# Starting the next stage's products inside the last attention half-head of a fp32 encoder layer

## The chip, the cores and the metric

One core of one Trainium2 chip runs the whole kernel in one launch. The metric is the device time of a run in microseconds (us); three runs of the kernel before were timed.

## The reference, cut to what matters

One encoder layer is applied to two request groups (512 tokens each, model width 1024) with shared weights, all in fp32:

```
h  = rmsnorm(x);  u = h @ w_in                        # one combined projection
hm = mlstm(q, k, v, gates)                            # branch A, both directions
y_m = (sigmoid(o) * rmsnorm(hm)) @ w_mo               # its projection, 1024 x 1024
p  = softmax(q k^T) per head;  o = p @ v              # branch B, 8 heads
y_a = o @ w_ao                                        # its projection, 1024 x 1024
x  = x + (sigmoid(g_m) * y_m + sigmoid(g_a) * y_a) @ w_out
x  = x + (silu(h2 @ w_gate) * (h2 @ w_up)) @ w_down   # FFN
x  = x + sigmoid(x @ w_ple_gate) * (p_l @ w_ple);  y = rmsnorm(x)
```

The stretch that matters is the end of branch B's attention and the start of `@ w_mo`, which is followed by `@ w_ao`.

## The kernel before, in words

Tiles are 128 partitions by 512 fp32 values. To keep fp32 accuracy every operand is split in two fp32r parts (`hi`, a cast on ScalarE; `lo`, source minus `hi` on VectorE, helper `lo_of`, line 155), and a product is three matmuls per 128 rows: hi·hi, hi·lo, lo·hi. `E`, `S`, `V`, `GP` are TensorE, ScalarE, VectorE and GpSimd.

**Attention.** There are 16 half-heads (`NU`; 8 heads times 2 groups). Each iteration `u` of the loop makes the scores of half-head u (`score`: five matmuls into a bank `sc` and a maximum on VectorE, for each of four query blocks), their exponentials (`expo`, ScalarE), transposes them (`turn`: four transposes into a bank `pt`, a cast `aph` on ScalarE; `turn_lo`: `apl` on VectorE), projects keys and queries of half-head u+1 (`proj_hi`, banks `pj`), and multiplies the weights of half-head u-1 with its values (`weigh`: eight `aph` and four `apl` matmuls into the bank `av`). Division by the softmax sum is done late for half-heads below `EVEN` = 14: `sums_row(u-1)` takes the reciprocals `rc`, transposes them on TensorE, and sends them through DRAM on GpSimd's DMA queue to come back broadcast as the tile `rb`; `weighed(u-1)` multiplies `av` by `rb` into `oz` at the end of the same iteration. Half-heads 14 and 15 divide `p` itself (`inverse`, `even`). The iteration of u = 15 has an order of its own (`if last:`) and a further one, u = 16, finishes it. Inside the loop `pinned` is set: compute instructions keep program order on each engine. Outside it a planner, which simulates a timeline, orders the instructions. `fill(...)` places small side jobs in the loop: splits of `hops`, the operands of the next stage.

**Next stage.** `w_mo` and then `w_ao` are applied as 2 x 2 block products with seven instead of eight block multiplications (class `Seven`). A quad is one such block pair: products P1, P2, P7, P6, P5, Q4, P3, each 12 matmuls, into banks b0, b1, b2; `w_mo` and `w_ao` have four quads each. Operand sums come from `Ops.part` (lines 934 to 956), weight sums from `Seven.source` (lines 999 to 1016), on VectorE for mo quads 0 and 3 and ao quad 0, on GpSimd for the others. `outputs` and `put_z` take results out of the banks. `chain` issues the products in an order with operands needed four products ahead. Weights of quad 0's P1, P2 and P7 are split during the loop (`ahead`); everything else of the chain is issued behind the loop (`issue_after(anchors)`). Before the chain the loop's banks are closed and six banks b0, b1, b2 and a spare are opened.

`hops`' raw tiles are loaded again for P5, Q4, P3 (`X2`), and for these its sums are made on GpSimd:

```
    hops.r, hops.t, hops.sums = {}, {}, lambda n: GP
    hops.raw = lambda g, k: load(hzd[g][k], X2, "x")
```

Of the kernel before, what the change touches and what calls it, by code (L numbers as in the profile page):

```python
# [17 lines left out]
NB = T // P  # L18
# [44 lines left out]
def encoder_kernel(ctx: ExitStack, tc: tile.TileContext, a):  # L63
# [56 lines left out]
            t = self.tags[n]  # L120
            return self.pool.tile([P, T], F32, name=nm(n), tag=t, bufs=self.bufs[t])

    pb = [None]

    def banks(name, bufs, **tags):
        if pb[0]:
            pb[0].ctx.close()
        pb[0] = Banks(name, bufs, tags) if name else None

    def bank(n="mm"):  # L130
        return pb[0](n)

    banks("P1", dict(mm=3, sc=2, tp=2, bc=1), mm="mm", sc="sT nm", tp="ssc tpc vtp ht", bc="rbc")
# [564 lines left out]
    M2.close()  # L698
    M1.close()
    MC.close()  # L700
    banks("P2", dict(pj=2, sc=3, tp=2, av=1), pj="mm pj", sc="sc", tp="pt", av="av")
    Q = Slots("Q", vt=1, rb=1, qkv=12, qst=4, p=4, ph=1, pl=1)
    QL = Slots("QL", lat=16)
    lat = {}
# [154 lines left out]
    def even(u, i):  # L859
        x = att[u]  # L860
        S.activation(out=x["p"][i], in_=x["p"][i], func=AF.Copy, scale=x["rc"][:, i : i + 1])
# [26 lines left out]
    def weigh(u):  # L888
        x, (vh, vl) = att[u], vn[u]
        ob = x["ob"] = bank("av")  # L890
        for j in range(NB):
            c = slice(j * P, (j + 1) * P)
            E.matmul(ob, vh[:, c], x["ph"][:, j], start=j == 0, stop=False)
            E.matmul(ob, vl[:, c], x["ph"][:, j], start=False, stop=False)
        for j in range(NB):
            E.matmul(ob, vh[:, j * P : (j + 1) * P], x["pl"][:, j], start=False, stop=j == NB - 1)

# [17 lines left out]
    late = {}  # L915
# [5 lines left out]
    class Ops:  # L921
# [2 lines left out]

        def __init__(self, raw, tmp, sums):
            self.raw, self.tmp, self.sums = raw, tmp, sums
            self.r, self.t, self.x = {}, {}, {}

        def get(self, n, k):
            if (n, k) not in self.r:  # L930
# [1 line left out]
            return self.r[n, k]  # L932

        def part(self, name, k):
            if name in ("P1", "P2", "P3"):
                return self.get({"P1": "a", "P2": "c", "P3": "d"}[name], k)
            add = self.sums(name).tensor_tensor
            if name == "P7":
                t = self.t[k] = self.tmp() or self.get("b", k)
                add(out=t, in0=self.get("b", k), in1=self.get("d", k), op=ALU.subtract)  # L940
            elif name == "P6":
                t = self.t[k]
                add(out=t, in0=t, in1=self.get("a", k), op=ALU.subtract)  # L943
            elif name == "P5":
                t = self.get("a", k)
                add(out=t, in0=t, in1=self.get("b", k), op=ALU.subtract)
            elif k in self.t:
                t = self.t[k]
                add(out=t, in0=t, in1=self.get("c", k), op=ALU.add)
            else:  # L950
                t = self.get("c", k)
                add(out=t, in0=t, in1=self.get("a", k), op=ALU.subtract)
                add(out=t, in0=t, in1=self.get("d", k), op=ALU.subtract)
            return t
# [27 lines left out]
    class Seven:  # L982
# [43 lines left out]
            self.w[name] = (hi, lo)  # L1026
            return (lambda: S.copy(hi, src)), (lambda: lo_of(lo, src, hi))

        def product(self, name):
            if name == "P6" and "P7" not in self.w:  # L1030
                self.w["P7"] = self.weights("P7")
            if name not in self.w:
                self.w[name] = self.weights(name)
            whi, wlo = self.w[name]
            b, first = {"P1": ("b1", 1), "P6": ("b1", 0), "P5": ("b1", 0), "P3": ("b1", 0), "P2": ("b0", 1),
                        "P7": ("b2", 1), "Q4": ("b2", 0)}[name]
            if first:
                self.bk[b] = bank(b)
            bk = self.bk[b]
            sk = dict(skip_group_check=True)  # L1040
            for k in range(self.kh):
                c = slice(k * P, (k + 1) * P)
                hi, lo = self.ops.x[name][k]
                E.matmul(bk, whi[:, c], hi, start=bool(first) and k == 0, stop=False, **sk)  # L1044
                E.matmul(bk, whi[:, c], lo, start=False, stop=False, **sk)  # L1045
                E.matmul(bk, wlo[:, c], hi, start=False, stop=k == self.kh - 1, **sk)  # L1046
            self.out(name, self.bk)

    def chain(quads, head=False, look=4, made=()):

        order = [(0, n) for n in ("P1", "P2", "P7")]
        if head:
            order = [(0, "P1"), (0, "P2"), (1, "P1"), (1, "P2"), (0, "P7"), (0, "P6"), (0, "P5"), (0, "Q4"), (1, "P7"), (0, "P3")]
        full = ("P6", "+P1", "P5", "+P2", "Q4", "+P7", "P3")
        ends = {
            len(quads) - 3: ("P6", "+P1", "P5", "+P2", "Q4", "P3"),
            len(quads) - 2: ("P6", "P7", "P5", "+P1", "Q4", "P3"),
            len(quads) - 1: ("P6", "P7", "P5", "P2", "Q4", "P3"),
        }
        for i in range(1 if head else 0, len(quads)):  # L1060
            for n in ends.get(i, full):
                if n[0] != "+":
                    order.append((i, n))
                elif i + 1 < len(quads):
                    order.append((i + 1, n[1:]))
        made = dict(made)

        def make(i):
            if i not in made:
                made[i] = quads[i][1]()  # L1070

        for at, (q, n) in enumerate(order):
            for i, m in order[at : at + look + 1]:
                quads[i][0].need(m)
            for i, _ in order[at : at + 2]:
                make(i)
            made[q].product(n)

    def outputs(put):
        keep = {}  # L1080

        def out(name, bk):
            if name in ("P1", "P6", "P5"):
                t = late["OP"]("ev", "u")
                S.copy(t, bk["b1"])  # L1085
                keep[name] = t
            if name in ("P2", "P5", "Q4"):
                t = keep[{"P2": "P1", "P5": "P5", "Q4": "P6"}[name]]
                b = bk["b0" if name == "P2" else "b2"]
                V.tensor_tensor(out=t, in0=b, in1=t, op=ALU.add if name == "P2" else ALU.subtract)  # L1090
                put({"P2": (0, 0), "P5": (1, 1), "Q4": (1, 0)}[name], t)
            if name == "P3":
                put((0, 1), bk["b1"])

        return out
# [77 lines left out]
    quads = [pair("mo", c, hops, put_z(c)) for c in range(4)]  # L1173
    ahead, anchors = {}, []

    def ahead_hi(n):
        hi, ahead[n] = pairs[0].ahead(n)
        hi()

    def ahead_lo(n):  # L1180
        ahead[n]()

    pinned[0] = True
    for u in range(NU + 1):
# [69 lines left out]
            todo_["f"] = [(ahead_lo, "P1")]  # L1254
        if u == 14:
            todo_ = {"mid": [(ahead_hi, "P2")], "d": [(ahead_lo, "P2")], "late": [(ahead_hi, "P7")], "f": [(ahead_lo, "P7")]}

        def odd(v, i):
            if EVEN <= v < NU - 1:
# [3 lines left out]
        if last:  # L1263
            score(u, 0)
            expo(u, 0)
            score(u, 1)
            turn(u - 1, 3)
            turn_lo(u - 1, 3)
            expo(u, 1)
            score(u, 2)  # L1270
            inverse(u, 0)
            even(u, 0)
            expo(u, 2)
            score(u, 3)
            inverse(u, 1)
            even(u, 1)
            expo(u, 3)
            for i in (2, 3):
                inverse(u, i)
                even(u, i)  # L1280
            v_split(u)
            weigh(u - 1)
            weighed(u - 1)
            for i in range(NB - 1):
                turn(u, i)
                turn_lo(u, i)
            continue
        if now:
            score(u, 0)
        fill("a")  # L1290
        if now:
            expo(u, 0)
# [8 lines left out]
        if then:  # L1301
            if u - 1 < EVEN:
                V.reciprocal(out=att[u - 1]["rc"], in_=att[u - 1]["den"])
            turn_lo(u - 1, 3)
        odd(u, 0)
        fill("c")
        if nxt:
            proj_hi(kn, u + 1, "ckv", 512)
            proj_lo(kn, u + 1)
        if then and u - 1 < EVEN:  # L1310
            sums_row(u - 1)
        odd(u, 1)
        fill("mid")
        fill("d")
        if then:
            weigh(u - 1)
        if now:
# [1 line left out]
            v_load(u + 1)  # L1319
            turn(u, 0)  # L1320
            turn_lo(u, 0)
            score(u, 2)
            turn(u, 1)
            expo(u, 2)
            turn_lo(u, 1)
# [7 lines left out]
            expo(u, 3)  # L1333
            turn_lo(u, 2)
            odd(u, 3)
            if then:
                weighed(u - 1)
            fill("f")
            fill("end")
        else:  # L1340
# [6 lines left out]
        if u == NU - 2:  # L1347
            QL.close()
            X2 = Slots("X2", "right", x=16)
    pinned[0] = False  # L1350
    hops.r, hops.t, hops.sums = {}, {}, lambda n: GP
    hops.raw = lambda g, k: load(hzd[g][k], X2, "x")
    Q.close()
    late["OP"] = Slots("OP", h=24, sg=4, ev=8)


    yr = [[None] * KD for _ in range(G)]
    banks("PF", dict(b1=3, b0=2, b2=2, sp=1), b0="b0", b1="b1", b2="b2", sp="sp")

    def put_y(c):  # L1360
        def put(at, t):
# [11 lines left out]
    with ExitStack() as behind:  # L1373
        for i in anchors:
            behind.enter_context(tc.issue_after(i))
        quads += [pair("ao", c, oops, put_y(c)) for c in range(4)]
        chain(quads, made=pairs)


    y = [[None] * KD for _ in range(G)]  # L1380
# [6 lines left out]
            V.scalar_tensor_tensor(out=lo, in0=t, scalar=0.5, in1=hi.bitcast(F32), op0=ALU.mult, op1=ALU.subtract)  # L1387
            y[g][k] = (hi, lo)
    OP = late["OP"]
    banks("P3", dict(mm=5, tp=1, bc=2), mm="mm", tp="ssc", bc="rbc")  # L1390

    class Sl:

# [423 lines left out]
```

## Time and profile before

| | |
|---|---|
| time, median of 3 runs | 1884.51 us (1883.68 to 1887.18) |
| profiled execution, its time | 1885.22 us |
| its span, first to last instruction | 1883.4 us |
| mean granted TensorE clock | 0.990 |
| PE (TensorE matmul) busy | 1831.4 us, 97% |
| VectorE (DVE) busy | 1238.8 us, 66% |
| ScalarE (ACT) busy | 860.7 us, 46% |
| GpSimd (POOL) busy | 393.3 us, 21% |

A timeline row has start (us from the span's start), duration, engine, line, operation, out<-in, count, and in brackets the idle time before it with what ended it. Rows merge neighbouring instructions of one kind. The page ends matmuls by a model, so the distance between the starts of two matmuls is the better measure of a matmul. In the loop most lines are L79, the helper that pins instructions, so tile names tell what is what. A row of a window has the busy time of each engine with its count of instructions, then the granted clock, the DMA share and GB/s.

### The profile page before, as it was taken

To read this page: it belongs to the slowest core of one execution; us is meant where nothing else is said; L and a number is where in the kernel's file an instruction comes from. 1 tells how busy PE (TensorE), PEld (TensorE's weight loads), DVE (VectorE), ACT (ScalarE), POOL (GpSimd) and SP (SyncE) were. 2 spreads that over 40 slices of the span, in tenths; PEclk is the share of its full clock that TensorE was granted. 3 is DMA by queue.
4 is the path that set the end of the run, shared out by engine and by line. 5 is a ranking of instruction groups with operands and counts; after the bars stand their busy time and mean duration, and the time that the engine had idled before them with its cause. 6 is when DMAs were issued, how large, how long until landed. Compare 5 with 4: busy or idle time off the path is not lost.

```text
span 1883.4 us, 24476 instructions
## 1 busy us (share of the span) xinstructions
PE 1831.4 (97%) x8815; PEld 1525.6 (81%) x8815; DVE 1238.8 (66%) x2084; ACT 860.7 (46%) x1690; POOL 393.3 (21%) x316
## 2 busy tenths in 40 slices
PE   9999999999999999987999999999999999999996
PEld 7889898988888777766878888888888888888786
DVE  6757576766532377768898588444444469878756
ACT  6255555653322566663444356333333344434433
POOL 0101000100000022215131002666556623111000
PEclk9999999999999999998999999999999999999998
DMA  4211212122333444354665342233222347533342
GB/s 165 66 59 49 69 44 79 44 69 79 121 113 111 156 124 118 96 201 157 193 209 155 120 145 84 101 115 110 96 97 95 130 142 237 166 129 101 105 136 95
DMA packets 104217, 220.43 MB, mean 117 GB/s; under 512 B 12584, under 2 KB 23264, under 8 KB 104096
## 3 DMA queue, kind: packets, MB, share of 16 engines
q1 hardware_dynamic: 88592, 166.15, 26.6%
q10 hardware_dynamic: 12096, 43.00, 7.1%
q0 software_dynamic: 3408, 9.73, 1.6%
q8 instruction: 69, 1.13, 0.3%
q14 instruction: 52, 0.43, 0.1%
HBM read 160.37 MB, written 54.26 MB: 114 GB/s over the span
## 4 chain that ended last, share of the span: by engine, by line
PE 47%; DVE 7%; issue 1%; ACT 1%; DMA 0%; ACTq 0%; DVEq 0%; POOLq 0%
PE b L1044 12%; PE b L1046 12%; PE b L1045 12%; PE mm L79 2%; DVE wp L155 2%; DVE xl L155 1%; PE mm L186 1%; PE mm L184 1%; PE mm L185 1%; PE mm L1606 1%; PE mm L1607 1%; PE mm L1608 1%; ACT p L79 0%; DVE x L1543 0%; DVE t L943 0%
## 5 line engine op out<-in xcount | busy, mean ns | idle before, releaser
L1046 PE MATMUL b<-xh,wp 128*128 128x512 f32 x1148 | 443.7, 391 | 12.2 <-DVE wp L155 12.2
L1045 PE MATMUL b<-xl,wp 128*128 128x512 f32 x1148 | 446.0, 390 | 2.1 <-DVE xl L155 2.1
L1044 PE MATMUL b<-xh,wp 128*128 128x512 f32 x1148 | 439.9, 391 | 6.5 <-ACT u L1085 2.3
L978 ACT CAST wp<-wst 128x512 fp32r<-128x512 f32 (+1 forms) x268 | 163.2, 612 | 301.0 <-PE b L1046 250.1
L155 DVE TENSOR_TENSOR wp<-wst,wp 128x512 fp32r<-128x512 f32 (+1 forms) x268 | 248.1, 928 | 68.9 <-ACT wp L978 68.7
L1046 PEld LDWEIGHTS b<-xh,wp 128*128 128x128 f32 x1148 | 216.3, 188 | 58.8 <-DVE wp L155 13.8
L1044 PEld LDWEIGHTS b<-xh,wp 128*128 128x128 f32 x1148 | 216.3, 188 | 57.1 <-ACT u L1085 5.5
L1045 PEld LDWEIGHTS b<-xl,wp 128*128 128x128 f32 x1148 | 216.1, 188 | 47.5 <-DVE xl L155 2.9
L184 PE MATMUL mm<-hh,whi 128*128 128x512 f32 x560 | 219.5, 392 | 0.9 <-DVE ql L155 0.9
L185 PE MATMUL mm<-hl,whi 128*128 128x512 f32 x560 | 219.2, 391 | 0.0
L186 PE MATMUL mm<-hh,wlo 128*128 128x512 f32 x560 | 218.9, 391 | 0.0
L1090 DVE TENSOR_TENSOR u<-b,u 128x512 f32<-128x512 f32 x90 | 61.8, 688 | 130.9 <-PE b L1046 82.1
L184 PEld LDWEIGHTS mm<-hh,whi 128*128 128x128 f32 x560 | 105.5, 188 | 23.0 <-DVE ql L155 1.3
L186 PEld LDWEIGHTS mm<-hh,wlo 128*128 128x128 f32 x560 | 105.6, 188 | 22.2 <-DVE wlo L155 0.3
L185 PEld LDWEIGHTS mm<-hl,whi 128*128 128x128 f32 x560 | 105.5, 188 | 21.3
L1005 POOL TENSOR_TENSOR s<-wst,wst 128x512 f32<-128x512 f32 (+1 forms) x29 | 45.3, 1562 | 308.7 <-DMA wst<-wd 137.0
L169 ACT CAST whi<-wst 128x1024 fp32r<-128x1024 f32 x59 | 62.0, 1050 | 98.6 <-PE mm L185 58.7
L1085 ACT COPY u<-b 128x512 f32<-128x512 f32 x90 | 50.7, 589 | 106.8 <-PE b L1046 64.0
L1505 POOL TENSOR_TENSOR sg<-sg,u 128x512 f32<-128x512 f32 x30 | 54.5, 1818 | 202.1 <-DVE u L1090 202.1
L155 DVE TENSOR_TENSOR wlo<-wst,whi 128x1024 fp32r<-128x1024 f32 (+2 forms) x62 | 75.0, 1212 | 14.5 <-ACT whi L169 13.6
L155 DVE TENSOR_TENSOR xl<-ld,xh 128x512 fp32r<-128x512 f32 x105 | 77.9, 769 | 1.0 <-ACT xh L1536 0.5
L383 DVE TENSOR_TENSOR tg<-rs,mm 128x512 f32<-128x512 f32 x32 | 22.0, 686 | 82.8 <-PE mm L186 77.6
(383 smaller groups left out, 3582.7 us busy)
## 6 DMA issues: line engine op xcount, KB each, us to landing
wst<-w SPq DMA_DIRECT2D x73, 512.0 KB, 3.2
wst<-w ACTq DMA_DIRECT2D x60, 512.0 KB, 3.8
ld<-actd SPq DMA_DIRECT2D x77, 256.0 KB, 3.4
actd<-t SPq DMA_DIRECT2D x40, 256.0 KB, 2.9
x<-x SPq DMA_DIRECT2D x32, 256.0 KB, 4.0
ld<-hzd SPq DMA_DIRECT2D x32, 256.0 KB, 3.0
wst<-wd ACTq DMA_DIRECT2D x16, 512.0 KB
actd<-sg SPq DMA_DIRECT2D x30, 256.0 KB, 2.3
```

The source lines that it names most:

```text
L155: e.tensor_tensor(out=out, in0=src, in1=hi.bitcast(F32), op=ALU.subtract)
L169: S.copy(hi[:, :n], st[:, :n])
L184: E.matmul(bk, whi[:, c], hi, start=k == 0, stop=False)
L185: E.matmul(bk, whi[:, c], lo, start=False, stop=False)
L186: last_mm[0] = E.matmul(bk, wlo[:, c], hi, start=False, stop=k == nk - 1)
L978: S.copy(hi, src)
L1044: E.matmul(bk, whi[:, c], hi, start=bool(first) and k == 0, stop=False, **sk)
L1045: E.matmul(bk, whi[:, c], lo, start=False, stop=False, **sk)
L1046: E.matmul(bk, wlo[:, c], hi, start=False, stop=k == self.kh - 1, **sk)
L1085: S.copy(t, bk["b1"])
L1090: V.tensor_tensor(out=t, in0=b, in1=t, op=ALU.add if name == "P2" else ALU.subtract)
L1505: e.tensor_tensor(out=sg[at], in0=sg[at], in1=t, op=ALU.mult)
```

## The change

The loop's two banks `pj` become two named banks `l0`, `l1` in a pool of their own (`low`), which stays open through the `w_mo` and `w_ao` stage. In iteration 15 and 16 the first four products of quad 0 (P1, P2, P7, P6) are issued between the attention's own TensorE work: P1 after the last score, P2 after the first transposed block, P7 after the second, P6 after the fourth. P1 and P6 go into `l0`, P7 into `l1`, P2 into a bank of the tag `sc`. With them come P1's and P2's results, P6's weights, the weights of quad 1's P1 and P2, and P5's four operand sums, all pinned. The chain then starts with quad 1's P1, P2, P7 and goes on with quad 0's P5, Q4, P3.

All sums of `hops` are now on VectorE (the line that switched them to GpSimd is gone). The 16 raw tiles are loaded at the end of iteration 14. In every iteration `sums_row` moves into `weigh`, between its eight `aph` and its four `apl` matmuls, and `weighed` moves from the end of the iteration to behind the first score of the next. For half-head 14 the third score moves ahead of `weigh`, and the normalisation of block 1 ahead of the key projection.

```diff
+    LOW = dict(mm=("l0", "l1"), pj=("l0", "l1"), b1=("l0", None, None), b2=("l1", None, None))
...
-    banks("P2", dict(pj=2, sc=3, tp=2, av=1), pj="mm pj", sc="sc", tp="pt", av="av")
+    banks("P2", dict(sc=3, tp=2, av=1), under=("l0", "l1"), sc="sc b0", tp="pt", av="av")
...
     def weigh(u):
...
+        if u < EVEN:
+            sums_row(u)
         for j in range(NB):
             E.matmul(ob, vh[:, j * P : (j + 1) * P], x["pl"][:, j], start=False, stop=j == NB - 1)
...
     def chain(quads, head=False, look=4, made=(), done=()):
...
-            for n in ends.get(i, full):
+            for n in ends.get(i, ("+P1", "+P2", "+P7", "P5", "Q4", "P3") if (i, "P6") in done else full):
...
+        order = [o for o in order if o not in done]
...
         if last:
...
             score(u, 1)
+            weighed(u - 2)
             turn(u - 1, 3)
...
             even(u, 1)
+            pre("P1", False)
             expo(u, 3)
...
             weigh(u - 1)
+            pairs[0].out("P1", pairs[0].bk)
+            ahead_hi("P6")
+            ahead_lo("P6")
+            turn(u, 0)
+            turn_lo(u, 0)
+            pre("P2")
+            turn(u, 1)
+            turn_lo(u, 1)
+            for k in range(4):
+                hops.pre["P5", k] = hops.part("P5", k)
             weighed(u - 1)
-            for i in range(NB - 1):
-                turn(u, i)
-                turn_lo(u, i)
+            pre("P7")
+            ahead_hi("P1", 1)
+            ahead_lo("P1", 1)
+            turn(u, 2)
+            turn_lo(u, 2)
+            ahead_hi("P2", 1)
+            ahead_lo("P2", 1)
             continue
         if now:
             score(u, 0)
+            if u > 1:
+                weighed(u - 2)
...
         odd(u, 0)
+        odd(u, 1)
         fill("c")
...
-        if then and u - 1 < EVEN:
-            sums_row(u - 1)
-        odd(u, 1)
         fill("mid")
         fill("d")
+        if now and u >= EVEN:
+            score(u, 2)
+        if u == NU:
+            pre("P6", False)
         if then:
             weigh(u - 1)
...
-            if then:
-                weighed(u - 1)
             fill("f")
...
             X2 = Slots("X2", "right", x=16)
+            hops.r, hops.t = {}, {}
+            hops.raw = lambda g, k: load(hzd[g][k], X2, "x")
+            for x in "abcd":
+                for k in range(4):
+                    hops.get(x, k)
     pinned[0] = False
-    hops.r, hops.t, hops.sums = {}, {}, lambda n: GP
...
-    banks("PF", dict(b1=3, b0=2, b2=2, sp=1), b0="b0", b1="b1", b2="b2", sp="sp")
+    banks("PF", dict(b1=2, b0=2, b2=2), b0="b0", b1="b1", b2="b2")
...
-        chain(quads, made=pairs)
+        pairs[0].out("P6", pairs[0].bk)
+        chain(quads, made=pairs, done=[(0, n) for n in ("P1", "P2", "P7", "P6")])
```

More of the change, by code (lines that the diff above doesn't have):

```diff
@@ L121, in __call__, with banks @@
             return self.pool.tile([P, T], F32, name=nm(n), tag=t, bufs=self.bufs[t])
-    pb = [None]
-    def banks(name, bufs, **tags):
+    pb, low, turns = [None], [None], {}
+    def banks(name, bufs, under=None, **tags):
         if pb[0]:
             pb[0].ctx.close()
+        if under is not None:
+            if low[0]:
+                low[0].ctx.close()
+            low[0] = Banks(name + "L", {n: 1 for n in under}, {n: n for n in under}) if under else None
+            turns.clear()
         pb[0] = Banks(name, bufs, tags) if name else None
+    LOW = dict(mm=("l0", "l1"), pj=("l0", "l1"), b1=("l0", None, None), b2=("l1", None, None))
     def bank(n="mm"):
+        if low[0] and n in LOW:
+            key = "pj" if n == "mm" else n
+            i = turns[key] = turns.get(key, -1) + 1
+            at = LOW[n][i % len(LOW[n])]
+            if at:
+                return low[0](at)
         return pb[0](n)
@@ L926, in __init__ @@
             self.raw, self.tmp, self.sums = raw, tmp, sums
-            self.r, self.t, self.x = {}, {}, {}
+            self.r, self.t, self.x, self.pre = {}, {}, {}, {}
         def get(self, n, k):
@@ L934, in part @@
         def part(self, name, k):
+            if (name, k) in self.pre:
+                return self.pre.pop((name, k))
             if name in ("P1", "P2", "P3"):
@@ L1027, in ahead, with product @@
             return (lambda: S.copy(hi, src)), (lambda: lo_of(lo, src, hi))
-        def product(self, name):
+        def product(self, name, out=True):
             if name == "P6" and "P7" not in self.w:
@@ L1046, in product, with chain @@
                 E.matmul(bk, wlo[:, c], hi, start=False, stop=k == self.kh - 1, **sk)
-            self.out(name, self.bk)
-    def chain(quads, head=False, look=4, made=()):
+            if out:
+                self.out(name, self.bk)
+    def chain(quads, head=False, look=4, made=(), done=()):
         order = [(0, n) for n in ("P1", "P2", "P7")]
@@ L1083, in out @@
             if name in ("P1", "P6", "P5"):
-                t = late["OP"]("ev", "u")
+                t = late["OP"]("ev", "u") if "OP" in late else Q("qkv", "u")
                 S.copy(t, bk["b1"])
@@ L1174, in encoder_kernel, with ahead_hi, ahead_lo @@
     ahead, anchors = {}, []
-    def ahead_hi(n):
-        hi, ahead[n] = pairs[0].ahead(n)
-        hi()
-    def ahead_lo(n):
-        ahead[n]()
+    def ahead_hi(n, i=0):
+        hi, ahead[i, n] = pairs[i].ahead(n)
+        hi()
+    def ahead_lo(n, i=0):
+        ahead[i, n]()
     pinned[0] = True
@@ L1256, in encoder_kernel @@
             todo_ = {"mid": [(ahead_hi, "P2")], "d": [(ahead_lo, "P2")], "late": [(ahead_hi, "P7")], "f": [(ahead_lo, "P7")]}
+        pre = lambda name, out=True: pairs[0].product(name, out)
         def odd(v, i):
@@ L1321, in encoder_kernel @@
             turn_lo(u, 0)
-            score(u, 2)
+            if u < EVEN:
+                score(u, 2)
             turn(u, 1)
@@ L1349, in encoder_kernel @@
             X2 = Slots("X2", "right", x=16)
+            hops.r, hops.t = {}, {}
[3 more added lines that the diff above has]
+                    hops.get(x, k)
     pinned[0] = False
-    hops.r, hops.t, hops.sums = {}, {}, lambda n: GP
-    hops.raw = lambda g, k: load(hzd[g][k], X2, "x")
     Q.close()
@@ L1389, in encoder_kernel @@
     OP = late["OP"]
-    banks("P3", dict(mm=5, tp=1, bc=2), mm="mm", tp="ssc", bc="rbc")
+    banks("P3", dict(mm=5, tp=1, bc=2), under=(), mm="mm", tp="ssc", bc="rbc")
     class Sl:
```

## The prediction

> **What bounds the kernel now.** I began with the page: which engine is full, and where it is not.
>
> ```profile
> PE 1831.4 (97%) x8815; PEld 1525.6 (81%) x8815; DVE 1238.8 (66%) x2084; ACT 860.7 (46%) x1690; POOL 393.3 (21%) x316
> ...
> PE   9999999999999999987999999999999999999996
> ...
> PEclk9999999999999999998999999999999999999998
> ```
>
> TensorE is the bound nearly everywhere, so only time in which it stands or runs at a lower clock can be won. Slices 18 and 19 (about 800 to 894 us) are the weakest in the middle, and the granted clock sinks there too. Next the waits of PE alone:
>
> ```profile
> PE b L1046 <- DVE wp L155: 12.2, 3, 10.9
> PE pt L79 <- DVE rc L79: 4.3, 11, 1.0
> PE pt L79 <- DVE apl L79: 3.0, 1, 3.0
> ...
> PE pt L79 <- ACT p L79: 1.4, 2, 0.7
> PE av L79 <- ACT aph L79: 0.9, 2, 0.7
> ```
>
> Columns: total, times, longest. The first row holds one wait of 10.9 us for a weight's lo part; the second is small and frequent, in the attention loop; the third is one wait of 3.0. The windows from the last half-head on place them (busy us of PE, PEld, DVE, ACT, POOL, then the clock):
>
> ```profile
> 836.00:848.00 12.00, 8.99 (x45) 6.98 (x43) 6.23 (x15) 8.62 (x19) 1.11 (x2) 0.89 0.91 327
> 848.00:855.00 7.00, 6.33 (x21) 4.99 (x21) 3.02 (x5) 2.11 (x4) 0.53 (x1) 0.70 0.08 9
> ...
> 862.00:874.00 12.00, 1.13 (x4) 0.88 (x4) 12.00 (x3) 0.27 (x1) 10.70 (x10) 0.66 0.17 45
> 874.00:880.00 6.00, 6.00 (x23) 4.84 (x22) 5.97 (x9) 0.00 (x0) 1.22 (x1) 0.82 0.07 24
> ...
> 945.00:955.00 10.00, 10.00 (x46) 8.11 (x44) 10.00 (x13) 5.06 (x10) 4.09 (x3) 1.00 0.33 92
> 955.00:970.00 15.00, 11.37 (x39) 7.91 (x39) 15.00 (x25) 7.78 (x16) 5.54 (x3) 0.89 0.90 296
> ```
>
> There are two holes, each followed by a stretch at half clock: one in the last half-head, one from 862 to 873. A third, smaller one at 955 to 970, where w_ao follows w_mo, has VectorE busy throughout. The timeline of PE shows the first two from inside:
>
> ```profile
> 839.42 0.39 PE L79 MATMUL av<-aph,vh 128*128 128x512 f32 x1
> ...
> 842.17 1.03 PE L79 MATMUL pt<-ident,p 128*128 128x128 f32 x8
> 846.20 1.97 PE L79 MATMUL pt<-ident,p 128*128 128x128 f32 x8 [2.99 <-DVE apl L79]
> 848.84 0.79 PE L79 MATMUL av<-aph,vh 128*128 128x512 f32 x1 [0.68 <-ACT aph L79]
> ...
> 853.28 0.40 PE L1044 MATMUL b<-xh,wp 128*128 128x512 f32 x1
> ...
> 861.45 0.39 PE L1044 MATMUL b<-xh,wp 128*128 128x512 f32 x1
> 861.67 0.39 PE L1045 MATMUL b<-xl,wp 128*128 128x512 f32 x1
> 872.93 0.80 PE L1046 MATMUL b<-xh,wp 128*128 128x512 f32 x1 [10.87 <-DVE wp L155]
> ...
> 876.83 0.39 PE L1044 MATMUL b<-xh,wp 128*128 128x512 f32 x1
> ```
>
> From 842 to 849 TensorE has only transposes, and each waits until ScalarE and VectorE have emptied one of two `pt` banks. From 853.28 it runs P1, P2, P7 (36 matmuls in 861.45 - 853.28 = 8.17 us, 0.227 each), starts P6, and stands from its third matmul on; P6 ends at 876.83. Why VectorE was late, from its own timeline and GpSimd's:
>
> ```profile
> 854.62 18.86 DVE L155 TENSOR_TENSOR wp<-wst,wp 128x512 fp32r<-128x512 f32 x2 [3.78 <-ACT wp L978]
> 873.40 0.68 DVE L155 TENSOR_TENSOR xl<-ld,xh 128x512 fp32r<-128x512 f32 x1
> ...
> 891.50 1.28 DVE L155 TENSOR_TENSOR xl<-ld,xh 128x512 fp32r<-128x512 f32 x2
> ...
> 855.03 5.04 POOL L946 TENSOR_TENSOR ld<-ld,ld 128x512 f32<-128x512 f32 x4
> 860.04 1.28 POOL L1005 TENSOR_TENSOR s<-wst,wst 128x512 f32<-128x512 f32 x1
> 861.29 4.93 POOL L952 TENSOR_TENSOR ld<-ld,ld 128x512 f32<-128x512 f32 x4
> 866.19 1.25 POOL L1006 TENSOR_TENSOR wst<-wst 128x512 f32<-128x512 f32 x1
> 867.41 4.91 POOL L953 TENSOR_TENSOR ld<-ld,ld 128x512 f32<-128x512 f32 x4
> ```
>
> Two VectorE instructions that take 1.28 us at 891.50 (0.60 each and a tail) took 18.86 while GpSimd ran 14 sums without a gap, and VectorE went on just after the last (867.41 + 4.91 = 872.32). The twelve operand sums (L946, L952, L953) are what the change moves.
>
> **The change part by part.** The sum is made against the profiled execution: 1885.22 us, span 1883.4, 1.8 around it. The median, 1884.51, lies 0.7 below.
>
> *Four products into the last half-head.* TensorE's work between 839.42 and the end of P6 stays: 48 product matmuls and 24 `av` matmuls at 0.227 (16.3) and 16 transposes. Eight of these came in about 0.95 us (842.17 to the idle that began at 846.20 - 2.99 = 843.21), so 1.9 for 16, 18.2 in all. Before it took 876.83 - 839.42 = 37.4. If nothing waits, 19.2 us go: about 7 from the first hole, 12 from the second with its half clock. Would something wait? In the new order VectorE has, from the last maximum to the last `apl`, v's lo part, P6's sum and lo, four `apl`, P2's result (two), four P5 sums and two weight lo parts: 15 instructions of 0.60, 9.0 us. TensorE's own row there is P1, two `av` sets (5.4), P2, P7, P6 and the transposes, 18. The tight place is the fourth transpose and the last `apl`: after P2's result, which VectorE can begin only when P2 is done (about 8.5 us in), come ten instructions, so about 15 us in; the `apl` half of the last `av` set starts about 16.5 us in. I take no wait, with about 1.5 us of cover. ScalarE adds two weight casts, P1's copy and P6's cast (0.6 each) within the same 18 us, in which it was busy 8.6 of 12: hidden. The 16 raw loads on SP are already issued around 832 before, so their place is free of cost; two more SP transfers (a gate tile in, a result out) go past them and are needed only late.
>
> *Operand sums on VectorE.* 12 x 0.60 = 7.2 us more VectorE, 15 us less GpSimd. P5's four lie in the 9.0 above. Q4's eight (4.8 us) can run once `apl` is over, while TensorE has 5.4 us of work left in P6 and `av`, and then P1, P2, P7 of quad 1 (8.2). What is needed by P3 of quad 0 is 12 operand lo parts, 8 sums, P3's weight sum, four weight lo parts and quad 1's P2 result (two): 27 x 0.60 = 16.2 us, from 15 to 31 us after the last score; P3 starts at 18.2 + 8.2 + 5.4 = 31.8. That just fits. But quad 1's four weight sums stay on GpSimd, their data long loaded, and they can begin when the last `oz` transfer is issued there, about 19 us in. Four sums at 1.25 are 5 us, and the rows above show VectorE held for the whole of such a run. I put a new wait of 4 us into the sum; ends: 0 (the sums fall into a gap of VectorE) and 9 (VectorE idles as much per product as it did before).
>
> The last end comes so: from 842.2 to 985 VectorE had some 19 us idle outside the hold. With 19 us less time, 17.6 less hold and 7.2 more work, about 7 to 10 may remain idle, so up to 9 turn into waits. The third hole (15 - 11.37 = 3.6 idle plus half clock) keeps its cause, a full VectorE; I leave it at 0, and 3 either way.
>
> On the hold the Trainium skill says otherwise than the row. By SBUF — State Buffer, section "Who interferes with whom", a VectorE instruction with two SBUF inputs and a GpSimd one that reads SBUF exclude each other for one whole instruction, whichever starts first. The 18.86 us of two instructions across 14 GpSimd ones do not agree with an exclusion by single instructions. By that rule the remaining four sums would delay single instructions by 1.25, the new wait would be nearer 2 than 4, and the total 1861, inside the forecast's own range.
>
> *The loop.* In 14 half-heads `sums_row`'s transpose stands in TensorE's order between the key projection and `weigh`, and waits for the reciprocal, which waits behind two maxima on VectorE:
>
> ```profile
> 797.44 0.40 PE L79 MATMUL pj<-ckvh,wlo 128*128 128x512 f32 x1
> 798.10 0.27 PE L79 MATMUL pt<-ident,rc 128*4 128x128 f32 x1 [0.27 <-DVE rc L79]
> ...
> 797.79 0.16 DVE L79 RECIPROCAL rc<-den 128x4 f32<-128x4 f32 x1
> ...
> 799.66 0.53 POOL L79 DMA_DIRECT2D rsd<-rb  x1 [3.32 <-ACT rb L79]
> 801.73 0.57 POOL L79 DMA_DIRECT2D rb<-rsd  x1 [1.54 <-PE pt L79]
> ...
> 807.54 0.68 DVE L79 TENSOR_TENSOR oz<-av,rb 128x512 f32<-128x512 f32 x1
> ...
> 812.41 0.53 POOL L79 DMA_DIRECT2D rsd<-rb  x1 [3.31 <-ACT rb L79]
> 817.94 0.57 POOL L79 DMA_DIRECT2D rb<-rsd  x1 [5.00 <-PE sc L79]
> ```
>
> 798.10 - 797.44 = 0.66 where a matmul takes 0.23: 0.43 lost, and about 1.1 at each of the two with the longest idle (0.8 and 1.0), so near 6.5 over 14. Behind eight `aph` matmuls (1.8 us) the reciprocal is long there. What is late next is the cast `aph` of the last block; it gains too, because the maximum of the next score is no longer queued behind `oz` (0.60). The transpose in its new place costs a change of kind, about 0.1 each. Net -5. Half-head 14's reordering takes most of the two remaining rows (`p` 0.7, `aph` 0.2): -1.
>
> What it delays: `rb`'s round trip starts about 1.5 us later, `oz` needs it about 0.6 later. Queue: the copy of `rb` on ScalarE, then on POOL `rsd`, `rb`, v's lo part. Issue to issue is 2.1 usually, 5.5 at 812.41; behind it `oz` came 5.8 us after the second issue. So most halves keep 1 to 2 us of cover, the one at 812 may hold VectorE for about 1 us; I take 0, at most 2 (two such halves).
>
> *Banks.* The two `pj` banks become `l0` and `l1`, turned in the same order; nothing in the chain waited for a bank before. 0.
>
> Sum: -19.2 + 4 - 5 - 1 = -21.2 of 1885.22 makes 1864.0; against the median 1863.3.
>
> **The rivals.** *VectorE becomes the bound after the loop.* For it: 15.00 of 15.00 us busy at 955, and 7.2 more work in less time. Against: its 17.6 us hold goes, more than it gets. At the upper end (9 instead of 4, the third hole 3 longer) the time is 1871; with a wait of 3 us in the last half-head as well (the cover of 1.5 gone) and the half clock behind it, which takes 0.30 of the 7 us at 848 to 855, it is 1871 + 3 + 2 = 1876.
>
> *The products do not fill the holes.* The waits at 843 and 862 would reappear elsewhere because what TensorE runs early it lacks later: only the loop's 6 us would be left, 1878.5, or nothing, 1884.5. Against: the second hole was no lack of TensorE work but a held VectorE, and the sums that held it leave GpSimd.
>
> *Slower: `rb` comes too late in every half-head.* One wait, VectorE at `oz`, which now stands between the two first maxima of the next half-head. Behind it in VectorE's order are the second maximum and the last `apl`, which TensorE needs in `weigh`, some 1.4 us of cover. To lose more than the 19 + 6 us gained, each of 14 halves must lose 1.8, so the round trip would have to be 1.5 + 1.4 + 1.8 = 4.7 us longer than today in all of them; one in 14 has a length like that now (812.41). At 2.2 each the time is about 1890.
>
> **How the numbers follow.** About 0.2%, 3.8 us, is what a measurement of this kernel tells from no change. My forecast (1857 to 1868): 0.62. VectorE the bound (1868 to 1877): 0.24. Holes reappear (1877 to 1888): 0.09, of which a third is within 0.2%. Slower: 0.05. Faster 0.91, same 0.04, slower 0.05. The range for 8 in 10: from 1857 (no new wait, the third hole 2 shorter) to 1873, two thirds of the way into the second case.
>
> **What would show it.** Right: no PE wait for `rc` in the loop, `pt<-ident,rc` behind `av` matmuls; from the last score to the end of P6 about 18 us, with the clock at 1.00; no VectorE instruction over 6 us near the end of the loop, and GpSimd with at most four sums in a row there. The 4 us: PE waits `b <- DVE` within 15 us behind the last `av`. Wrong: VectorE waits for `rb` of 1 us and more in most halves; PE idle before `pt` or `av` in half-head 15; a hole at w_mo to w_ao that grew beyond 6 us.

## The result, and the profile after

The changed kernel takes 1859.57 us (median; 1857.04 to 1863.45) against 1884.14 us before: ratio 0.9868, 95% interval 0.9847 to 0.9889. The forecast was 1863.3, range 1857 to 1873. The profiled execution is the slowest of the after runs: 1863.45 us, span 1861.6. Its page, the lines that answer to those shown of before:

```profile
PE 1825.2 (98%) x8815; PEld 1523.9 (82%) x8815; DVE 1227.3 (66%) x2096; ACT 860.9 (46%) x1690; POOL 389.6 (21%) x304
...
PE   9999999999999999999999999999999999999996
...
PEclk9999999999999999999999999999999999999998
```

The weak slices in the middle are gone, in PE and in the clock. VectorE has 12 instructions more and GpSimd 12 fewer: the moved sums. The timeline of PE through the last half-head, and the windows from the last score on:

```profile
830.35 0.39 PE L79 MATMUL sc<-qh,ql 128*128 128x512 f32 x1
830.58 0.39 PE L79 MATMUL l<-xh,wp 128*128 128x512 f32 x1
...
842.44 1.03 PE L79 MATMUL pt<-ident,p 128*128 128x128 f32 x8
843.23 0.48 PE L79 MATMUL l<-xh,wp 128*128 128x512 f32 x1
...
848.78 0.39 PE L1061 MATMUL b<-xh,wp 128*128 128x512 f32 x1
...
855.94 0.50 PE L1061 MATMUL b<-xh,wp 128*128 128x512 f32 x1 [1.33 <-ACT wp L995]
...
863.01 0.50 PE L1063 MATMUL b<-xh,wp 128*128 128x512 f32 x1 [1.08 <-DVE wp L168]
...
868.21 0.50 PE L1062 MATMUL l<-xl,wp 128*128 128x512 f32 x1 [1.95 <-DVE xl L168]
```

```profile
830.60:848.80 18.20, 18.20 (x90) 15.12 (x89) 13.17 (x26) 9.18 (x18) 0.55 (x1) 1.00 0.65 226
...
854.00:873.00 19.00, 14.64 (x55) 10.91 (x54) 17.18 (x21) 10.08 (x19) 10.34 (x7) 0.91 0.78 265
873.00:930.00 57.00, 57.00 (x253) 47.18 (x252) 46.61 (x77) 26.58 (x49) 8.19 (x3) 1.00 0.57 179
930.00:950.00 20.00, 16.42 (x64) 12.51 (x64) 20.00 (x30) 9.84 (x18) 8.25 (x4) 0.91 0.76 257
```

From P1's first matmul (830.58) TensorE does not stand once until quad 1's P1 begins at 848.78: 18.2 us for what took 37.4. Then come three waits of 1 to 2 us with a short half clock (854 to 873, PE 14.64 of 19), and the hole at w_mo to w_ao is still there (930 to 950). Why the three waits, from VectorE's and GpSimd's timelines:

```profile
846.18 2.49 DVE L969 TENSOR_TENSOR ld<-ld,ld 128x512 f32<-128x512 f32 x4
848.59 0.69 DVE L1032 TENSOR_TENSOR wst<-wst 128x512 f32<-128x512 f32 x1
849.19 2.50 DVE L970 TENSOR_TENSOR ld<-ld,ld 128x512 f32<-128x512 f32 x4
...
857.07 1.78 DVE L168 TENSOR_TENSOR xl<-ld,xh 128x512 fp32r<-128x512 f32 x1
858.77 1.78 DVE L168 TENSOR_TENSOR wp<-wst,wp 128x512 fp32r<-128x512 f32 x1
...
850.53 4.70 POOL L1022 TENSOR_TENSOR s<-wst,wst 128x512 f32<-128x512 f32 x1
855.31 1.28 POOL L1023 TENSOR_TENSOR wst<-wst 128x512 f32<-128x512 f32 x1
856.67 1.63 POOL L1025 TENSOR_TENSOR wst<-wst,wst 128x512 f32<-128x512 f32 x1
```

Here the hold is the other way round: VectorE runs Q4's sums without a gap from 846.18, and GpSimd's sum for quad 1's P7, 1.28 us elsewhere, takes 4.70: VectorE's run, Q4's sums and then lo parts, ends at 854.10, and the sum at 855.23. After that the two take turns, and VectorE's 0.69 becomes 1.78. The cast that PE waits for at 855.94 is of this very sum; the waits at 863.01 and 868.21 are for lo parts that VectorE made late.

To compare the kernels I use two stretches of each profile, taken from the starts of PE's matmuls: the loop (first to last matmul of a score) and the stage (last matmul of a score to the first matmul of w_out).

| kernel | median us | ratio to before (95%) | loop us | stage us |
|---|---|---|---|---|
| before | 1883 to 1885 | 1 | 202.1 | 186.5 |
| changed | 1859.6 | 0.9868 (0.9847 to 0.9889) | 195.1 | 173.6 |
| changed, once more | 1860.4 | 0.9872 (0.9858 to 0.9887) | 194.4 | 171.4 |
| sums_on_vector | 1875.1 | 0.9957 (0.9940 to 0.9974) | 201.5 | 179.2 |
| loop_only | 1876.4 | 0.9960 (0.9945 to 0.9975) | 194.6 | 186.9 |
| after_sums_on_gpsimd | 1870.1 | 0.9928 (0.9910 to 0.9946) | 195.6 | 182.9 |
| no_early_products | 1867.6 | 0.9909 (0.9894 to 0.9924) | 194.4 | 177.0 |
| before_p5_on_gpsimd | 1878.4 | 0.9977 (0.9963 to 0.9991) | 201.5 | 181.7 |
| sums_row_only | 1882.3 | 0.9995 (0.9986 to 1.0005) | 202.6 | 187.7 |
| weighed_only | 1883.5 | 1.0006 (0.9995 to 1.0017) | 203.0 | 186.2 |
| after_quad1_on_vector | 1857.3 | 0.9856 (0.9841 to 0.9870) | 194.4 | 166.4 |
| the same, again | 1858.8 | 0.9866 (0.9849 to 0.9882) | 193.4 | 167.3 |
| quad1_on_vector_look6 | 1859.0 | 0.9867 (0.9852 to 0.9881) | 194.3 | 169.2 |
| quads12_on_vector | 1854.8 | 0.9848 (0.9833 to 0.9862) | 194.4 | 165.9 |

The rest of the program keeps its length (857 to 860 us from w_out on). The start of the loop lies between 633.5 and 637.0 us in these profiles, 637.0 in the profile of before and 635.2 in that of after: 1.8 of the 21.8 us between the two spans lies ahead of the loop. Kernels that leave that part as before spread as much (633.5 to 637.0), so I don't count it to the change.

### The profile page after: what moved, and what is told of

It is laid out like the page before. It is cut to its first block, busy times and chain, and to the rows that moved or that the text cites. A ratio compares the mean times of both kernels' runs of the same rounds, so it can differ in the third digit from the quotient of the medians.

```text
span 1861.6 us, 24494 instructions
## 1 busy us (share of the span) xinstructions
PE 1825.2 (98%) x8815; PEld 1523.9 (82%) x8815; DVE 1227.3 (66%) x2096; ACT 860.9 (46%) x1690; POOL 389.6 (21%) x304
## 4 chain that ended last, share of the span: by engine, by line
PE 45%; DVE 6%; issue 3%; DMA 1%; ACT 1%; POOL 0%; ACTq 0%; DVEq 0%; POOLq 0%
PE b L1061 11%; PE b L1063 11%; PE b L1062 11%; PE mm L79 2%; DVE xl L168 2%; PE mm L199 1%; PE mm L197 1%; PE mm L198 1%; DVE wp L168 1%; PE mm L1651 1%; PE mm L1649 1%; PE mm L1650 1%; PE l L1062 0%; PE l L1063 0%; PE l L1061 0%
## 5 line engine op out<-in xcount | busy, mean ns | idle before, releaser
L1061 PE MATMUL b<-xh,wp 128*128 128x512 f32 x1072 | 411.4, 392 | 9.3 <-ACT wp L995 5.5
L1062 PE MATMUL b<-xl,wp 128*128 128x512 f32 x1072 | 417.3, 390 | 0.8 <-DVE xl L168 0.8
L1063 PE MATMUL b<-xh,wp 128*128 128x512 f32 x1072 | 413.5, 390 | 1.6 <-DVE wp L168 1.6
L168 DVE TENSOR_TENSOR wp<-wst,wp 128x512 fp32r<-128x512 f32 (+1 forms) x265 | 225.4, 853 | 61.2 <-ACT wp L995 61.1
L1061 PEld LDWEIGHTS b<-xh,wp 128*128 128x128 f32 x1072 | 201.8, 188 | 57.1 <-ACT wp L995 8.5
L1063 PEld LDWEIGHTS b<-xh,wp 128*128 128x128 f32 x1072 | 201.9, 188 | 44.8 <-DVE wp L168 2.6
L197 PE MATMUL mm<-hh,whi 128*128 128x512 f32 x464 | 181.4, 391 | 0.0
L198 PE MATMUL mm<-hl,whi 128*128 128x512 f32 x464 | 181.1, 390 | 0.0
L199 PE MATMUL mm<-hh,wlo 128*128 128x512 f32 x464 | 180.9, 391 | 0.0
L199 PEld LDWEIGHTS mm<-hh,wlo 128*128 128x128 f32 x464 | 87.1, 188 | 18.1 <-DVE wlo L168 0.3
L197 PEld LDWEIGHTS mm<-hh,whi 128*128 128x128 f32 x464 | 87.1, 188 | 17.7 <-DVE to L396 0.2
L554 PE MATMUL mm<-whi,hh 128*128 128x256 f32 x256 | 72.0, 283 | 0.6 <-DVE cu L396 0.6
```

The source lines that it names most:

```text
L168: e.tensor_tensor(out=out, in0=src, in1=hi.bitcast(F32), op=ALU.subtract)
L197: E.matmul(bk, whi[:, c], hi, start=k == 0, stop=False)
L198: E.matmul(bk, whi[:, c], lo, start=False, stop=False)
L199: last_mm[0] = E.matmul(bk, wlo[:, c], hi, start=False, stop=k == nk - 1)
L554: E.matmul(out, hi[:, tb], whi[:, n], start=k == 0, stop=False)
```

## The experiments

**Operand sums alone.** `sums_on_vector`:

```diff
-    hops.r, hops.t, hops.sums = {}, {}, lambda n: GP
+    hops.r, hops.t = {}, {}
```

> The kernel before with one edit: the twelve operand sums of P5 and Q4 behind the loop stay on VectorE. Theory (GpSimd's run of sums held VectorE): the instruction of 18.9 us is gone, the PE wait of 10.9 us at 862 falls to 0 to 4 us, the half clock behind it too; the hole before 853 and the loop stay. 1871 to 1876 us. Rival 1 (only products moved ahead pay, because VectorE was late with its own work): the wait stays at 7 us or more, as VectorE has 7.2 us more to do; 1880 to 1886. Rival 2 (exclusion by single instructions, so GpSimd's sums cost VectorE little): no change, 1883 to 1887.

Measured 1875.1; the stage is 7.3 us shorter. Waits of PE behind the loop, and GpSimd:

```profile
PE b L1044 <- ACT wp L978: 2.0, 1, 2.0
PE b L1046 <- DVE wp L155: 0.8, 1, 0.8
```

```profile
851.10 8.87 POOL L1005 TENSOR_TENSOR s<-wst,wst 128x512 f32<-128x512 f32 x1
```

The wait of 10.9 is down to 0.8, so it was GpSimd's run; both rivals fall. Of the 12 us some go again to a wait of 2.0 and to VectorE's added work, and now VectorE holds one GpSimd sum for 8.87 us.

**The dose.** `before_p5_on_gpsimd` leaves P5's four sums on GpSimd and has Q4's eight on VectorE:

```diff
-    hops.r, hops.t, hops.sums = {}, {}, lambda n: GP
+    hops.r, hops.t, hops.sums = {}, {}, lambda n: GP if n == "P5" else V
```

> The kernel before with Q4's eight sums on VectorE and only P5's four on GpSimd, a dose of the hold. Theory (VectorE is held for as long as GpSimd's run is gapless): one VectorE instruction of 5 to 8 us at the end of the loop (four operand sums and up to two weight sums of 1.25) where the kernel before has 18.3, the PE hole there 0 to 3 us, and the stretch from the last score to the first matmul of w_out 179 to 182 us (186.5 before, 179.2 with all sums on VectorE). Rival (exclusion by single instructions): no VectorE instruction over 2 us there.

```profile
850.46 8.96 DVE L155 TENSOR_TENSOR wp<-wst,wp 128x512 fp32r<-128x512 f32 x2 [3.81 <-ACT wp L978]
...
850.88 5.05 POOL L946 TENSOR_TENSOR ld<-ld,ld 128x512 f32<-128x512 f32 x4
855.89 1.28 POOL L1005 TENSOR_TENSOR s<-wst,wst 128x512 f32<-128x512 f32 x1
857.25 1.62 POOL L1006 TENSOR_TENSOR wst<-wst 128x512 f32<-128x512 f32 x1
```

The first of the two VectorE instructions takes 7.26 us: it starts 0.42 ahead of GpSimd's run of five sums without a gap and ends 0.56 behind it. It gets through between the fifth sum (ends at 857.17) and the sixth (857.25), and the sixth, 1.25 in a run, takes 1.62. The PE wait is 4.3, longer than the 0 to 3 expected; the stage, 181.7, is in its range.

**The changed kernel with its sums on GpSimd.** `after_sums_on_gpsimd`:

```diff
-            hops.r, hops.t = {}, {}
+            hops.r, hops.t, hops.sums = {}, {}, lambda n: GP
```

> The changed kernel with the twelve operand sums of P5 and Q4 on GpSimd again. Theory (a gapless GpSimd run holds VectorE, and the early products do not cover that): a PE hole of 5 to 12 us returns between the last av matmuls and P3 of quad 0, with half clock behind it; 1866 to 1873. Rival (the early products give enough work ahead, the place of the sums does not matter): 1858 to 1862, no hole longer than the 2 us that the changed kernel has there.

```profile
864.55 0.79 PE L1062 MATMUL l<-xl,wp 128*128 128x512 f32 x1 [8.86 <-DVE xl L168]
...
851.69 12.81 DVE L168 TENSOR_TENSOR xl<-ld,xh 128x512 fp32r<-128x512 f32 x1 [4.44 <-ACT xh L979]
...
851.61 5.02 POOL L969 TENSOR_TENSOR ld<-ld,ld 128x512 f32<-128x512 f32 x4
...
862.69 1.25 POOL L1023 TENSOR_TENSOR wst<-wst 128x512 f32<-128x512 f32 x1
```

1870.1, some 10 us above the changed kernel, with a hole of 8.9 us. Early products do not cover a held VectorE. (The profiled execution, 1874.6, is the slowest of its four.) In three kernels the hold grows with the run: 5 sums 7.26 us, 10 sums 12.81, 14 sums 18.26 (the longer of the two instructions in the row of 18.86), 1.2 us a sum on average. It ends 0.55 us after the run, about what such an instruction takes by itself (0.60).

**No early products.** `no_early_products` is the kernel before with the loop part (next) and the sums' edit.

> The kernel before with the loop part and with all sums on VectorE, but without the four early products and what goes with them. Theory (the early products fill the first hole, 7 us, and give VectorE's moved sums their cover, some 4 us): 1867 to 1870, so 8 to 11 us above the changed kernel. Rival (the early products are worth only the first hole or less, the moved sums did the rest): 1862 to 1866.

1867.6, in the theory's range; 7 to 8 us above the changed kernel, a little under its 8 to 11, and the stage 3.4 to 5.6 longer. PE waits from 832 to 880:

```profile
PE pt L79 <- DVE apl L79: 2.7, 1, 2.7
PE b L1046 <- ACT wp L980: 2.0, 1, 2.0
PE av L79 <- ACT aph L79: 0.7, 1, 0.7
```

The first hole is back. Four kernels with the loop part (`loop_only`, described next, this one, `after_sums_on_gpsimd`, the changed one) separate the other two parts. In the stage the moved sums alone give 9.9 us (186.9 to 177.0), the early products alone 4.0 (to 182.9), both 13.3 to 15.5. By the ratios of the medians it is 9.6 and 6.0 alone and 16.6 to 17.3 together, where one ratio is known to 3 or 4 us. So the two add up; that one makes room for the other, as the theory's 4 us of cover has it, is not shown.

**The loop alone.** `loop_only` takes from the change (cut; the remarks behind `#` are mine):

```diff
+        if u < EVEN:
+            sums_row(u)                 # in weigh, between aph and apl matmuls
...
+            if u > 1:
+                weighed(u - 2)          # behind score(u, 0)
...
-            if then:
-                weighed(u - 1)
...
+        if now and u >= EVEN:
+            score(u, 2)                 # ahead of weigh; odd(u, 1) ahead of fill("c")
```

> The kernel before with the loop part alone: sums_row inside weigh, weighed behind the next first score, half-head 14's two reorderings; no early products, sums on GpSimd as before. Theory: PE waits for rc go and half-head 14 loses its two waits, 6 to 7 us, so 1877 to 1878.5. Rival (rb comes too late behind its later start): VectorE waits for rb of 1 us and more in several halves and less than 3 us gained, 1881 or more.

1876.4, the loop 7.6 us shorter. All that is left of PE's waits in it:

```profile
PE sc L79 <- DVE ql L79: 1.2, 1, 1.2
PE pt L79 <- ACT p L79: 0.7, 1, 0.7
```

The waits for `rc` are gone, and so are half-head 14's two small ones (0.7 and 0.2). The wait of 1.2 for `ql`, at the last half-head's scores, is new. It is not from half-head 14's reordering: `sums_row_only`, which lacks that, has it too (1.2).

**Its two halves.** `sums_row_only` moves `sums_row` and leaves `weighed`:

> The kernel before with sums_row inside weigh, weighed left at the end of its iteration. Theory of the prediction (the wait for the reciprocal goes, but rb comes 1.5 us later and oz has not moved, so VectorE waits for rb in some halves; the cast aph keeps its old time and becomes the next wait of PE): 2 to 5 us of the 7 in the loop, waits of oz for rb of 0.3 to 1.5 us in several halves, PE waits av from aph. Rival (the place of the transpose is all that matters): 6 to 7.5 us, as with both.

`weighed_only` moves `weighed` and leaves `sums_row`:

> The kernel before with weighed behind the next first score, sums_row left ahead of weigh. Theory (with oz behind the first maximum, the second maximum and the reciprocal keep their time, so PE still waits for rc): 0 to 2 us gained in the loop. Rival (the order on VectorE alone pays, the reciprocal comes 0.6 us sooner): 4 us and more.

Both leave half-head 14 as it was. Neither gains anything: 202.6 and 203.0 us of loop against 202.1. Waits of the first, then of the second:

```profile
PE av L79 <- ACT aph L79: 5.3, 5, 2.5
DVE oz L79 <- DMA rb<-rsd: 4.3, 3, 2.2
```

```profile
PE pt L79 <- DVE rc L79: 6.6, 13, 0.9
```

Without `weighed` moved, `rb` is late for three `oz`, and `aph` takes the place of `rc` as PE's wait. The kind of wait is what theory said, its size was not: I had expected 2 to 5 us of gain. Without `sums_row` moved, the wait for `rc` grows from 4.3 to 6.6. Of the two only the pair pays.

**The waits that are left.** `after_quad1_on_vector` adds `("mo", 1)`, `quads12_on_vector` also `("mo", 2)`, to the pairs whose weight sums are on VectorE:

```diff
-        e = V if (kind, c) in (("mo", 0), ("mo", 3), ("ao", 0)) else GP
+        e = V if (kind, c) in (("mo", 0), ("mo", 1), ("mo", 3), ("ao", 0)) else GP
```

> The changed kernel with quad 1's four weight sums on VectorE too. Theory (the three waits of 1.1 to 2.0 us at 854 to 868 come from VectorE and GpSimd excluding each other there: 4.7 us for a sum of 1.3 on GpSimd, 1.8 us for instructions of 0.7 on VectorE): those waits and the half clock behind them shrink from 6 us to 1 to 3, time 3 to 5 us below the changed kernel, 1855 to 1857. Rival (VectorE is simply full there, so 2.4 us more work makes it worse): same waits or longer, 1860 to 1864.

> The changed kernel once more, for a comparison on one chip with the next two: 1857 to 1863 us, ratio to before 0.986 to 0.988. Theory: the waits behind the last av matmuls depend on whether VectorE's or GpSimd's run comes first, so their length may differ from the first profile (6 us there) by a few us.

> Quad 1's weight sums on VectorE, once more beside the changed kernel on the same chip. Theory (exclusion between VectorE and GpSimd makes the waits): 2 to 5 us below the changed kernel. Rival (the first difference was the chip's): within 1 us of it.

On one chip 1858.8 against 1860.4 for the changed kernel, ratios 0.9866 and 0.9872: 1.6 us, between what theory and rival had, and too near for the times to tell. In the profiles the stage is 166.4 and 167.3 against 173.6 and 171.4, and up to 930 us PE has one wait of 1.1 (the run again) where the changed kernel, once more, has these:

```profile
PE b L1061 <- ACT wp L995: 1.3, 1, 1.3
PE b L1063 <- DVE wp L168: 1.1, 1, 1.1
```

So GpSimd out of the way is worth 1.3 us of waits there on one chip, and 3.7 between the first profiles of the two kernels (4.36 to 0.6). Most of the rest of the 4.1 us between the two stages on one chip lies at the third hole, where the clock in 925 to 955 is 1.00 instead of 0.94 and the waits 0.7 shorter; why is not shown.

> The changed kernel with the weight sums of quads 1 and 2 on VectorE. Theory (a GpSimd sum of 1.3 us that VectorE's run stretches to 5.9 delays quad 2's P7 by about 1 us): the wait of 0.8 to 1.3 us near 859 goes, the stretch from the last score to w_out 165 to 166.5 us (166.4 and 167.3 with quad 1 alone), time 1855 to 1858. Rival (VectorE gets too full for w_ao's operands): the hole at w_mo to w_ao grows, 168 us or more.

1854.8 (1852.7 to 1856.6), ratio 0.9848, the lowest here. Its times lie below all of the changed kernel's, but it ran on another chip than that kernel, once more, and the intervals of the two ratios (0.9833 to 0.9862; 0.9858 to 0.9887) just overlap. The wait near 859 is 0.5 and the stage 165.9, against 171.4 and 173.6. More work on the fuller engine did not make the stage longer, it made it shorter.

**Looking further ahead.** `quad1_on_vector_look6` changes `look` from 4 to 6 in that chain.

> As the run before it, and the chain of w_mo and w_ao prepares operands six products ahead instead of four. Theory (the hole at w_mo to w_ao comes from VectorE, which is full there but has gaps some 30 us earlier): part of the work moves into these gaps, the hole of about 4 us shrinks to 0 to 2, 2 to 4 us less than without it. Rival (operands taken earlier only push results and weights back on VectorE and ScalarE): same or up to 4 us more.

The rival's number holds: 1859.0, and the stage, 169.2, is longer than the 167.3 beside it. Waits at the hole, 925 to 945, and a window around it, with look 6 and then with 4:

```profile
PE b L1061 <- ACT u L1104: 2.2, 1, 2.2
PE b L1063 <- DVE wp L168: 0.9, 1, 0.9
...
925.00:955.00 30.00, 26.89 (x104) 21.22 (x103) 30.00 (x39) 10.45 (x19) 15.28 (x8) 0.89 0.65 202
```

```profile
PE b L1061 <- ACT wp L995: 4.4, 2, 3.2
...
925.00:955.00 30.00, 25.58 (x112) 20.31 (x111) 30.00 (x41) 11.30 (x22) 16.37 (x7) 1.00 0.66 219
```

The hole changed its releaser and is 1.3 us shorter, and PE's waits behind 840 are fewer in all (5.0 us, 6.2 with look 4). The stage is longer because the clock behind the hole was 0.89 instead of 1.00. That is neither the theory's gain nor the rival's waits. Why a hole of 4.4 us kept the clock and one of 3.1 did not, and what would close the hole, stays open.

## Why the prediction was right

- *Four products early, -19.2.* Measured 37.4 - 18.2 = 19.2, with no wait and the clock at 1.00; the order of VectorE's work that the cover of 1.5 us was worked out from held: the last `apl` is done at 846.27, its matmuls start at 847.88. (The two times behind "about 0.95 us" for eight transposes are 1.04 apart; that moves the sum by 0.2.)
- *Operand sums, +4 of new wait.* The waits between the last `av` and quad 0's P3 came to 1.33 + 1.08 + 1.95 and a short half clock in one profile, some 6 us, and to 1.3 + 1.1 at full clock in the other. The 4 lies between, but the step behind it is wrong, so that fit is luck: I had GpSimd's four weight sums holding VectorE, and it was VectorE's gapless run that held GpSimd's first sum (4.70), with turns of 1.78 after it. That the meeting of the two makes these waits is shown by `after_quad1_on_vector`, where they shrank as the sums left GpSimd.
- *The hold itself.* The reading that GpSimd's run, not VectorE's own lateness, made the second hole is shown by `sums_on_vector`. The Trainium skill (SBUF — State Buffer, "Who interferes with whom") has the exclusion last for one instruction, whichever starts first. The turns of 1.6 to 1.8 us agree with that, the runs do not: 7.26, 12.81 and 18.26 us for one VectorE instruction, 8.87 for one GpSimd sum. Nor did the first to start win: before the change, VectorE's held instruction starts at 854.62, the run of sums at 855.03 (what GpSimd did just ahead was to issue a transfer, and no run tells whether that counts). The total by that rule, 1861, lay nearer the result than mine; that is no evidence for it, the runs with sums moved one way and the other decide.
- *The loop, -5 and -1.* Measured -7.0 in the first profile, -7.6 in `loop_only`, 1.0 to 1.6 more than the -6. Half-head 14's two waits went as forecast; what was too small is the term for `rc`, though a wait of 1.3 for `ql` came with it. Its own figures, 12 halves at 0.43 and two at 1.1, make 7.4 and not 6.5, and -6.0 net instead of -5. The prediction priced the pair and named `aph` as next; that each half alone is worth nothing it did not say.
- *`rb` later.* `oz` waited 0.7 us once, at 815, and 0.06 once (before: 1.2 once): as expected, and the slower rival is out.
- *The third hole, 0.* PE waits 3.6 us there after, as before (11.37 busy of 15), and 5.2 in the second profile of the changed kernel, within the 3 either way. VectorE is still full at that place (20.00 of 20).
- *The sum.* -21.2 forecast; -24.6 between the medians, -19.9 in loop and stage between the two profiles, -22.8 with the second profile of the changed kernel. In the first profile the new wait, 2 us over its 4, outweighs what the loop gave more; in the second the loop and the new wait together are 3 us better than forecast and the third hole 1.6 worse. The rest of the -24.6 lies outside these stretches or between executions, and I can't place it.

## What to carry to other kernels

When one engine's instruction takes many times its usual length, look at what its neighbour ran during it: moving that neighbour's work can be worth more than the work costs where it goes. Look also at whether a hole is a lack of work or a held engine: filling it with later work did not remove the hold, and the two remedies simply added up. A transpose moved behind the matmuls that hide its wait paid here only when the other work that the same place waits for moved too.

## What the runs showed of the hardware that I had not expected

VectorE and GpSimd sums with two SBUF inputs keep each other out, and instructions back to back keep the other engine waiting through many of them, in both directions: VectorE was held for 7.26, 12.81 and 18.26 us by 5, 10 and 14 sums of about 1.25 us; one GpSimd sum took 4.70 to 10.05 us under VectorE's runs. In one run VectorE got in at a gap of 0.08 us between two GpSimd sums. Once the held one had got in, the two took turns, at 1.6 to 1.8 us for either's instruction.

VectorE's run lets GpSimd in without a gap too, at an instruction with one input in a bank of TensorE. In `sums_on_vector`, where a GpSimd sum is held from 851.10:

```profile
858.12 0.69 DVE L155 TENSOR_TENSOR xl<-ld,xh 128x512 fp32r<-128x512 f32 x1
858.72 0.69 DVE L1090 TENSOR_TENSOR u<-b,u 128x512 f32<-128x512 f32 x1
859.32 1.20 DVE L155 TENSOR_TENSOR xl<-ld,xh 128x512 fp32r<-128x512 f32 x1
```

VectorE has no gap there, and the held sum ends at 859.97, 1.25 us after `u<-b,u` starts. Behind the last score the 14 profiles hold 51 GpSimd sums that took over 2 us. 49 of them end 1.25 us (within 0.04) after the start of such a VectorE instruction, the other two after VectorE's run stopped, as at 854.10 in the changed kernel. So how long a GpSimd sum is held follows from where VectorE's next bank read stands.
